# Output projection by tokens, routing by halves and 2 MB expert loads in a one-core hybrid decoder layer

## The chip, the core and the metric

The kernel runs on one core of one Trainium2 chip. It is one program that computes a whole decoder layer (token mixer, then a mixture of 32 experts) for 256 tokens of width 1024. The metric is the device time of one execution, in microseconds. Compute engines are TensorE (PE; its weight loads are shown apart as PEld), VectorE (DVE), ScalarE (ACT) and GpSimd (POOL); SyncE (SP) issues nearly all the loads from HBM, in one fixed order.

## The reference, cut to what matters

```python
# T = 256 tokens, D_MODEL = 1024, 32 experts of width 512, all f32
merged = sigmoid(gate_a) * (o_attn @ w_branch_attn) + sigmoid(gate_r) * (o_rwkv @ w_branch_rwkv)
h = h + gt1 * (merged @ w_out)                       # the output projection, 1024 x 1024
xn2 = _rmsnorm(h, moe_norm_g) * (1.0 + sc2) + sh2
# _hier_moe(xn2):
p_group = softmax(xt @ wg_router)                    # 4 groups, the best one is taken
e_logits = xt @ we_router + e_bias                   # 32 experts, the best 2 in that group
hdn = silu(xt @ wg) * (xt @ wu)                      # per expert: gate, up ...
acc = acc + cw[:, None] * (hdn @ wd)                 # ... and down
h = h + gt2 * moe
```

The output projection's result decides the routing, and the routing decides which tokens each expert sees. The weights of the experts are 3 x 2 MB for each of 32, 192 MiB (201 MB) together.

## The kernel before

**Token mixer.** Generators for modulation, selection, RWKV, attention and gates are stepped by a string written by hand (`ORDER`); each step issues a few instructions. Products are made nearly in f32: every operand is cast to the reduced type fp32r as a high part, and what the cast left is a low part. `split` (L526 to L529) does it for a tile of weights, with a cast on ACT or POOL and a subtraction on DVE or POOL (`SPLIT` says by letters which, "AP" being cast on ACT and subtraction on POOL). `mm3` (L539 to L541) then makes three products: high by high, high by low, low by high.

**Output projection.** `w_out` comes in four loads of 1 MB, `("wo", j)`, each with two of the eight slices k of the contraction. Slices are split one ahead of the other into two pairs of tiles. For every k, `out_part(m, k, w)` makes the part of one block m of 128 outputs for all 256 tokens: the weights that TensorE holds are `w[0][:, m:1024:8]`, every eighth column of the split slice, and the 256 tokens are streamed. The result is h transposed (outputs on partitions, tokens along the row), in eight blocks of 256 columns in PSUM, which four products with zeros (`zero`) open. For the last two slices the loop over m is outside, so that blocks come ready one by one; router products (`logits`, L1479), sums of squares (`squares`, L1485) and transposes back to tokens on partitions (`turn`, L1491, into `h2`) follow. To start with, the input x had been transposed into `h` in `rwkv()` (L1072).

**Routing.** A chain of small instructions on DVE (L1562 to L1593) makes 1/rms by iteration, normalises the router's sums, takes the best group and the two best experts for all 256 tokens at once; three products (L1597, L1598) rank the tokens of each expert, `places` builds a one-hot table (L1694, L1697), and `gather` (L1624) collects by products up to 32 tokens for each of four experts. `begin` (L1714) adds h into the four PSUM banks of the final sum by four 512-column products with the identity.

**Experts.** They run in eight quads of four: gate and up by `rows_in` and `row_in` (L1639, L1645: the 32 gathered tokens are the weights, 512 columns of an expert's matrix stream), down by L1666. SP's loads go in a fixed order; `pump` issues the next as soon as the arena in SBUF has a free place of its size (keeping `RESERVE` columns free in each stage), and `done` frees a tile and calls `pump`. Expert matrices of quads 0 and 1 are loaded in halves of 1 MB; from quad 2 on in 2 MB (`WHOLE = 2`), but for `down` in the last quad. The first quad's first gate halves come by slices k (`row_in`), so that each product frees some of them. Extra room comes when the split tiles of the mixer are given up (pools `more0` and `more`).

Of the kernel before, what the change touches and what calls it, by code (L numbers as in the profile page):

```python
# [18 lines left out]
D = 1024  # L19
# [34 lines left out]
RESERVE = (29696, 17408, 24576, 4096, 0)  # L54
# [4 lines left out]
SPLIT = (('PD', 'PD', 'AP', 'AD'), ('PD', 'PD', 'AP', 'AD'), ('PP', 'PP', 'AD', 'AD'), ('AD', 'AP', 'AD', 'AD'), ('AD', 'PD', 'AP', 'PD'))  # L59
PRIO = ('mod', 'sel', 'rwkv', 'attn', 'gate')  # L60
ORDER = 'mrrrrrrrrmmrmrrmrrrrrmrrrarmmrmrrmmmmrrrmarmmrmarrramrmamrrsraarmmraarmarmmaasrmmsaaaasmmsrarssrarrsaraarrararrsaasrsasssagrarssssgsraargrsrgsrsgggsrrmgmmgsmrrrrggrgrsgrrggggrsaggrrrggaggrgrrrgagagaggagaaggggaaaggaaggggaggagaggaaaagaaggaaaaaggaaaaaaggagagggggggggg'
LORD = (0, 1, 2, 3, 4, 5, 6, 7, 8, 9, 10, 13, 15, 11, 12, 14, 17, 16, 18, 23, 19, 20, 21, 22, 24, 28, 25, 27, 29, 26, 30, 31, 32, 33, 34, 35, 36, 37, 38, 44, 39, 40, 41, 51, 45, 49, 42, 48, 43, 47, 52, 46, 50)
INFO = []
QUADS = NE // 4
WHOLE = 2
# [91 lines left out]
def layer_kernel(tc, I, out, dbg=None):  # L157
# [21 lines left out]
    B = Arena(fr.__enter__().tile([128, nB], F32R, name="split"), nB)  # L179
# [83 lines left out]
    def whole(n, q):  # L263

        return q >= WHOLE and not (n == "ed" and q == QUADS - 1)

# [70 lines left out]
    nc.sync.dma_start(out=wrt[:, :, 0:4], in_=I["router_group_w"][0].rearrange("(p k) n -> p k n", p=128))  # L337
    nc.sync.dma_start(out=wrt[:, :, 4:36], in_=I["router_expert_w"][0].rearrange("(p k) n -> p k n", p=128))
# [100 lines left out]
    xhi = B.get(8, T)  # L439
    xlo = B.get(8, T)  # L440

    def mod_half(hf):
# [32 lines left out]
        def rest(kk, eng):  # L475
            k = 4 * hf + kk
            eng.tensor_sub(xlo[:, k, :], xn[:, kk, :], xhi[:, k, :].bitcast(F32))


        for kk in range(2):  # L480
            nc.scalar.activation(xhi[:, 4 * hf + 2 + kk, :], src(2 + kk), AF.Identity, scale=mo[:, 1, 2 + kk:3 + kk],
                                 bias=mo[:, 0, 2 + kk:3 + kk])
            normed(kk)
            nc.scalar.copy(xhi[:, 4 * hf + kk, :], xn[:, kk, :])  # L484
# [58 lines left out]
    def proj_cols(key, c0, ps, last=False):  # L543

        for k2 in range(2):
# [3 lines left out]
            for kk in range(4):  # L549
                k = 4 * k2 + kk  # L550
                mm3(ps, (h[:, kk, :], l[:, kk, :]), (xhi[:, k, :], xlo[:, k, :]), k == 0, k == 7)
# [12 lines left out]
    def rows_part(key, hf, mp, n, fin, i0=0):  # L564

        ps = PS(WIDE)
        for m in range(n):
# [3 lines left out]
            for i, (a, b) in enumerate(((h, xhi), (l, xhi), (h, xlo))):  # L571
                for kk in KORD:
                    nc.tensor.matmul(p, a[:, kk, :], b[:, 4 * hf + kk, :], start=(i == 0 and kk == KORD[0]),  # L573
                                     stop=(i == 2 and kk == KORD[-1]))
# [63 lines left out]
    h = io = io1 = zero = trib = selb = trib_ = selb_ = mg = m8 = rs2 = sel = comb = rk = rt = hsq = hx = None  # L638

    def rwkv():  # L640
# [396 lines left out]
        nonlocal h, io, io1, zero, trib, selb, trib_, selb_, mg, m8, rs2, sel, comb, rk, rt, hsq, hx  # L1037
        h = M(8, T)
        hx = M(1024)
        hsq = hx[:, 0:768].rearrange("p (k t) -> p k t", k=3)  # L1040
        rt = hx[:, 768:1024]
        xt = M(2, D)
        nc.sync.dma_start(out=xt, in_=I["x"][0].rearrange("(a p) d -> p a d", p=128))
# [4 lines left out]
        zero = M(64)  # L1048
        nc.gpsimd.memset(zero, 0.0)
# [17 lines left out]

        for q in range(4):
            ps = PS()
            for kk in range(2):  # L1070
                for a in range(2):
                    nc.tensor.transpose(ps[:, kk * 256 + a * 128:kk * 256 + a * 128 + 128],  # L1072
                                        xt[:, a, 2 * q + kk:D:8], ident)
            nc.scalar.copy(h[:, 2 * q:2 * q + 2, :], ps.rearrange(v2, a=2))
            yield 0.5
        A.free(xt)
# [884 lines left out]
```

## Time and the profile before

| what | before |
|---|---|
| median of 3 runs | 801.64 us (800.87 to 804.71) |
| the profiled execution | 800.6 us, its span 798.8 us |
| mean granted TensorE clock | 0.921 of 2.4 GHz |
| busy: PE, PEld, DVE, ACT, POOL | 83%, 47%, 35%, 21%, 17% of the span |
| moved by DMA | 261.36 MB, mean 327 GB/s |

The span is the time between the first and the last instruction that the profiler saw. PE's busy share is an upper figure, since a pipelined product's end is modelled; how far apart products start says more. All times below are microseconds from the start of the span.

### The profile page before, as it was taken

To read this page: it belongs to the slowest core of one execution; us is meant where nothing else is said; L and a number is where in the kernel's file an instruction comes from. 1 tells how busy PE (TensorE), PEld (TensorE's weight loads), DVE (VectorE), ACT (ScalarE), POOL (GpSimd) and SP (SyncE) were. 2 spreads that over 40 slices of the span, in tenths; PEclk is the share of its full clock that TensorE was granted. 3 is DMA by queue.
4 is the path that set the end of the run, shared out by engine and by line. 5 is a ranking of instruction groups with operands and counts; after the bars stand their busy time and mean duration, and the time that the engine had idled before them with its cause. 6 is when DMAs were issued, how large, how long until landed. Compare 5 with 4: busy or idle time off the path is not lost.

```text
span 798.8 us, 11321 instructions
## 1 busy us (share of the span) xinstructions
PE 660.6 (83%) x4657; PEld 379.2 (47%) x4657; DVE 277.0 (35%) x665; ACT 164.9 (21%) x350; POOL 132.9 (17%) x171
## 2 busy tenths in 40 slices
PE   5898988899999999989998586777676777778567
PEld 2785657568889889974442131131131132222112
DVE  2577799887255645141211061011010010010001
ACT  2445412343176631031110010010010010000000
POOL 1456643322235133220000000000000000000000
PEclk9899999999999999989999698889889899889879
DMA  9997476552758368249999999999999999999995
GB/s 334 392 309 245 143 261 241 175 192 81 244 191 284 106 235 344 66 162 377 422 420 428 427 425 431 425 427 432 425 428 429 427 427 428 427 428 427 427 394 201
DMA packets 53796, 261.36 MB, mean 327 GB/s; under 512 B 6864, under 2 KB 18128, under 8 KB 37360
## 3 DMA queue, kind: packets, MB, share of 16 engines
q1 hardware_dynamic: 53456, 260.11, 82.4%
q8 instruction: 37, 0.61, 0.3%
q10 hardware_dynamic: 288, 0.52, 0.2%
q14 instruction: 15, 0.12, 0.0%
HBM read 259.57 MB, written 1.05 MB: 326 GB/s over the span
## 4 chain that ended last, share of the span: by engine, by line
DMA 33%; PE 27%; DVE 1%; SPq 1%; POOL 1%; ACT 0%; issue 0%; ACTq 0%; POOLq 0%
DMA more<-in_expert_w_up_dram 12%; DMA more<-in_expert_w_down_dram 11%; DMA more<-in_expert_w_gate_dram 10%; PE ps_e L1639 10%; PE ps_e L1666 4%; PE ps_e L1624 2%; PE ps_a L541 1%; PE ps_a L539 1%; PE ps_a L540 1%; PE acc L1721 1%; PE ps_e L1673 1%; PE acc L1714 1%; SPq L296 1%; PE ps_r L539 0%; PE ps_r L540 0%; PE ps_r L541 0%
## 5 line engine op out<-in xcount | busy, mean ns | idle before, releaser
L1639 PE MATMUL ps_e<-arena,more 128*32 128x512 f32 x456 | 83.9, 693 | 24.2 <-DMA arena<-in_expert_w_gate_dram 18.3
L1639 PE MATMUL ps_e<-arena 128*32 128x512 f32 x424 | 81.9, 709 | 22.4 <-DMA arena<-in_expert_w_up_dram 12.4
L1666 PE MATMUL ps_e<-arena 128*32 128x512 f32 x360 | 73.5, 659 | 17.6 <-DMA arena<-in_expert_w_down_dram 12.9
L529 DVE TENSOR_TENSOR split<-arena,split 128x512 fp32r<-128x512 f32 x77 | 61.3, 805 | 57.7 <-POOL split L526 29.1
L528 ACT CAST split<-arena 128x512 fp32r<-128x512 f32 x71 | 43.3, 618 | 74.6 <-PE ps_g L540 29.3
L573 PE MATMUL ps_a<-split 128*128 128x256 f32 x360 | 52.1, 303 | 3.3 <-ACT split L484 1.9
L1650 ACT ACTIVATE arena<-ps_e 128x512 f32<-128x512 f32 x8 | 4.8, 597 | 239.2 <-PE ps_e L1639 239.2
L1651 DVE SCALAR_TENSOR_TENSOR arena<-arena,ps_e 128x512 f32<-128x512 f32 x8 | 5.5, 688 | 140.0 <-ACT arena L1650 140.0
L573 PEld LDWEIGHTS ps_a<-split 128*128 128x128 f32 x360 | 47.8, 204 | 12.6 <-issue 6.8
L529 POOL TENSOR_TENSOR split<-arena,split 128x512 fp32r<-128x512 f32 x33 | 45.3, 1372 | 48.6 <-ACT split L528 25.5
L1704 POOL TENSOR_TENSOR arena<-arena 128x256 f32<-128x256 f32 x8 | 4.9, 616 | 283.4 <-PE ps_e L1707 281.8
L1683 DVE TENSOR_TENSOR arena<-ps_e,more 128x512 f32<-128x512 f32 (+1 forms) x17 | 11.8, 692 | 112.9 <-PE ps_e L1666 103.7
L1639 PEld LDWEIGHTS ps_e<-arena,more 128*32 128x32 f32 x456 | 18.6, 126 | 60.8 <-issue 27.7
L1639 PEld LDWEIGHTS ps_e<-arena 128*32 128x32 f32 x424 | 18.2, 128 | 56.4 <-issue 26.1
L1666 PE MATMUL ps_e<-more,arena 128*32 128x512 f32 x88 | 34.9, 632 | 8.4 <-DMA more<-in_expert_w_down_dram 7.7
L526 POOL TENSOR_SCALAR split<-arena 128x512 fp32r<-128x512 f32 x39 | 26.8, 688 | 82.9 <-PE ps_r L540 23.8
L1639 PE MATMUL ps_e<-more,arena 128*32 128x512 f32 x56 | 31.3, 722 | 10.7 <-DMA more<-in_expert_w_gate_dram 10.7
L1666 PEld LDWEIGHTS ps_e<-arena 128*32 128x32 f32 x360 | 16.5, 117 | 49.0 <-issue 22.5
L1639 PE MATMUL ps_e<-more,more 128*32 128x512 f32 x56 | 30.3, 702 | 10.6 <-DMA more<-in_expert_w_up_dram 10.6
L1652 DVE SCALAR_TENSOR_TENSOR arena<-arena,ps_e 128x512 f32<-128x512 f32 x8 | 8.2, 1029 | 87.3 <-PE ps_e L1639 87.3
L539 PE MATMUL ps_g<-split 128*128 128x256 f32 x128 | 38.3, 299 | 0.0
L1624 PEld LDWEIGHTS ps_e<-arena,more 128*128 128x128 f32 x256 | 30.9, 196 | 12.9 <-issue 8.2
(379 smaller groups left out, 1263.0 us busy)
## 6 DMA issues: line engine op xcount, KB each, us to landing
arena<-in_expert_w_gate_dram SPq DMA_DIRECT2D x21, 2048.0 KB, 22.3
arena<-in_expert_w_up_dram SPq DMA_DIRECT2D x21, 2048.0 KB, 23.6
arena<-in_expert_w_down_dram SPq DMA_DIRECT2D x17, 2048.0 KB, 21.1
arena<-in_w_in_dram SPq DMA_DIRECT2D x18, 1024.0 KB, 8.1
arena<-in_expert_w_down_dram SPq DMA_DIRECT2D x18, 1024.0 KB, 17.9
arena<-in_ada_w_dram SPq DMA_DIRECT2D x16, 1024.0 KB, 6.8
arena<-in_expert_w_up_dram SPq DMA_DIRECT2D x14, 1024.0 KB, 9.8
arena<-in_expert_w_gate_dram SPq DMA_DIRECT2D x12, 1024.0 KB, 8.3
```

Source lines behind the costliest of these rows:

```text
L296: nc.sync.dma_start(out=dst, in_=src)
L526: nc.gpsimd.tensor_scalar(h, w, 1.0, 0.0, op0=OP.mult, op1=OP.add)
L528: nc.scalar.copy(h, w)
L529: (nc.gpsimd if p[1] == "P" else nc.vector).tensor_sub(l, w, h.bitcast(F32))
L539: nc.tensor.matmul(ps, l[0], r[0], start=start, stop=False)
L540: nc.tensor.matmul(ps, l[0], r[1], start=False, stop=False)
L573: nc.tensor.matmul(p, a[:, kk, :], b[:, 4 * hf + kk, :], start=(i == 0 and kk == KORD[0]), stop=(i == 2 and kk == KORD[-1]))
L1624: nc.tensor.matmul(ps[:, n * kk:n * kk + n], h2[:, a, 2 * k2 + kk, :], oh(a), start=(a == 0), stop=(a == 1))
L1639: nc.tensor.matmul(ps[32 * g:32 * g + 32, :], xg[:, k, 32 * g:32 * g + 32], w[:, k - 4 * i, :], start=(k == 0), stop=(k == 7))
L1652: nc.vector.scalar_tensor_tensor(hidb[0:r].rearrange("p (j q) -> p q j", j=4), thb[0:r].rearrange("p (q j) -> p q j", j=4), 0.5, psu[0:r, ...
L1666: nc.tensor.matmul(pss[c][32 * g:32 * g + 32, :], hTb[:, j, 32 * g:32 * g + 32], w[:, j - 2 * i, 512 * c:512 * c + 512], start=(j == 0), s ...
L1683: nc.vector.tensor_mul(Yb[0:r, c:c + 512], ps[0:r], gt2[0][0:r, g:g + 512])
```

## The change

It has four parts. **By tokens:** in the output projection the merged input (`xhi`, `xlo`, 128 tokens of it) is now what TensorE holds, and 512 columns of `w_out` stream; the result has tokens on partitions, the same way round as x, which is loaded straight into `h2`. The transposes of x, the products with zeros and the transposes back fall away; gt1 is now spread over the partitions as a row (two f32 products of 512 columns and two ACT copies more, `mod_bcast`). **By halves:** `LAST` is an order written by hand for the end of the projection: O for the products of one 128-token half and one 512-column half, T for four transposes, L for router products, N (`root`) for 1/rms and R (`route`) for the choice of one half of the tokens. W is an extra bf16 product of 512 columns that nobody reads. `CHAIN` places the four products of `begin` in the routing; `weights` (the softmax of the chosen) goes behind the first expert products and `prepare` for quad 1 behind quad 0's `down`. **Loads:** 2 MB from expert 4, counted from 0, on (`WHOLE = 1`), and in the last quad `up` in halves as well. **Memory and tables:** the split pool is cut so that 4096 columns come free after `("wo", 1)` and 6144 at the end, where before it was 2048 ahead of the projection and the rest at the end; `ORDER`, `LORD` (the order of the mixer's loads), `SPLIT` and `RESERVE` have new numbers.

```diff
-RESERVE = (29696, 17408, 24576, 4096, 0)
+RESERVE = (25600, 17408, 20480, 4096, 0)
-WHOLE = 2
+WHOLE = 1
+CHAIN = ('01', '2', '', '3', '', '')
+LAST = 'O00 O01 O10 O11 O20 O21 T00 O30 T01 L00 O31 L01 N0 R0 T10 W2 T11 N1 W1 L10 L11'
...
-        return q >= WHOLE and not (n == "ed" and q == QUADS - 1)
+        return q >= WHOLE and not (n != "eg" and q == QUADS - 1)
...
-    def out_part(m, k, w):
-        mm3(block(m), (w[0][:, m:1024:8], w[1][:, m:1024:8]), (mh[:, k, :], ml[:, k, :]), k == 0 and m > 5,
-            k == 7 and m not in (0, 2, 4))
+    def leave_room(name, cols, *before, **k):
+        for p in before:
+            p.__exit__(None, None, None)
+        state["more"].append(Arena(pool(name=name, bufs=1, **k).tile([128, cols], F32, name="more" + name), cols))
+        pump()
+
+    def out_part(a, c, k, w):
+        s = slice(128 * a, 128 * a + 128)
+        mm3(pso[2 * a + c], (xhi(k, s), xlo(k, s)), (w[0][:, 512 * c:512 * c + 512], w[1][:, 512 * c:512 * c + 512]), k == 0,
+            k == 7)
+
+    def residual(a, c):
+
+        hv = h2[:, a, 512 * c:512 * c + 512]
+        for o in (0, 256) if a and c else (0,):
+            r = slice(o, o + 256 if a and c else 512)
+            nc.vector.tensor_mul(tb[c][:, r], pso[2 * a + c][:, r], gt1[:, 512 * c:512 * c + 512][:, r])
+            (nc.vector if a else nc.gpsimd).tensor_add(hv[:, r], hv[:, r], tb[c][:, r])
+        nc.scalar.activation(tb[c], hv, AF.Square, scale=1.0 / 32, accum_out=st[:, 2 * c + a:2 * c + a + 1])
...
+            if kk:
+                done(("wo", j))
+            for n in range(4 if j < 3 else 0):
+                out_part(n // 2, n % 2, 2 * j + kk, ws[kk])
+        if j == 1:
+            leave_room("sb1", nB2 + 2048, fr2, fr1, side="right")
...
+    def warm(ps, n):
+
+        for _ in range(n):
+            nc.tensor.matmul(ps, trib[:, 0:128], trib[:, None, 0:256].to_broadcast([128, 2, 256]), start=True, stop=True)
...
+    after_last(ranks)
+    for f in CHAIN[1]:
+        after_last(lambda: begin(int(f)) if f != "W" else warm(psw, 1))
...
-                        fetch(0, [k2])
-                        for k in () if i else (2 * k2, 2 * k2 + 1):
-                            row_in(ps, XGb[0], need(("row", k)), k)
-                            done(("row", k))
+                        after_last(lambda: fetch(0, [k2]))
+                        for f in CHAIN[2 + k2]:
+                            after_last(lambda: begin(int(f)) if f != "W" else warm(psw, 1))
+                    for k in range(0 if i else 4):
+                        after_last(lambda: row_in(ps, XGb[0], need(("row", k)), k))
+                        done(("row", k))
```

On PE, the end of the output projection before: the last two products of the projection (split weights, 256 tokens), router products with 36 columns, transposes L1491, sums of squares L1485, and the ranks L1597.

```order
L540 MATMUL ps_r<-split 128x256
L541 MATMUL ps_r<-split 128x256
L1479 MATMUL ps_r<-arena 128x36 x4
L1491 MATMUL ps_g<-arena 128x128 x4
L1479 MATMUL ps_r<-arena 128x36 x4
L1491 MATMUL ps_g<-arena 128x128 x2
L1485 MATMUL ps_r<-arena 128x1 x6
L1491 MATMUL ps_g<-arena 128x128 x10
L1597 LDWEIGHTS arena
L1597 MATMUL ps_g<-arena 128x32
```

The same place after the change: L550 to L552 are the three products of the projection, L1498 transposes, L1505 router products, L1570 the products that nobody reads.

```order
L552 MATMUL ps_r<-split 128x512
L1498 MATMUL ps_g<-arena 128x128 x4
L1505 MATMUL ps_r<-arena 128x36 x4
L550 MATMUL ps_r<-split 128x512
L551 MATMUL ps_r<-split 128x512
L552 MATMUL ps_r<-split 128x512
L1505 MATMUL ps_r<-arena 128x36 x4
L1498 MATMUL ps_g<-arena 128x128 x4
L1570 LDWEIGHTS arena
L1570 MATMUL ps_r<-arena 128x512
```

Products have twice the columns; the transposes of the first half of the tokens and half of its router products stand before the projection's last products, and products that nobody reads stand behind them. Further on, between the ranks and the first expert products on PE, before:

```order
L1714 MATMUL acc_3382<-more,arena 128x512
L1624 MATMUL ps_e<-arena,more 128x128 x4
L1714 MATMUL acc_3383<-more,arena 128x512
L1645 MATMUL ps_e<-arena 32x512 x8
L1624 MATMUL ps_e<-arena,more 128x128 x7
```

And after (L1599 is `begin`, L1653 `gather`, L1674 `row_in`):

```order
L1599 MATMUL acc_3232<-arena 128x512
L1653 MATMUL ps_e<-arena 128x128 x8
L1599 MATMUL acc_3233<-arena 128x512
L1674 MATMUL ps_e<-arena 32x512 x16
L1653 MATMUL ps_e<-arena 128x128 x8
```

Eight gathering products, not four, now stand ahead of the first expert product, and all sixteen products by slices follow in one piece. On SP, the loads around this place after the change (`moresb_3057` and `moresb_3219` are the two rooms that come free):

```order
L300 DMA moresb_3057<-in_expert_w_down_dram 128x2048
L300 DMA arena<-in_expert_w_down_dram 128x2048 x2
L300 DMA moresb_3219<-in_expert_w_down_dram 128x2048 x3
L300 DMA arena<-in_expert_w_down_dram 128x2048 x2
L300 DMA arena<-in_expert_w_gate_dram 128x4096 x4
```

Before, the last of these rows stood as eight loads of 128x2048; the number of 1 MB pieces ahead of it is the same, 24, of which 22 don't wait for an expert product, in both kernels.

## Rows read from the trace of the kernel before

**Rows 1.** Page: GB/s in 40 slices of the span; the chain that ended last.

```profile
GB/s 334 392 309 245 143 261 241 175 192 81 244 191 284 106 235 344 66 162 377 422 420 428 427 425 431 425 427 432 425 428 429 427 427 428 427 428 427 427 394 201
DMA 33%; PE 27%; DVE 1%; SPq 1%; POOL 1%; ACT 0%; issue 0%; ACTq 0%; POOLq 0%
```

**Rows 2.** SP's DMA issues in order of time: start, us, queue, line, tile.

```profile
363.94 1.27 SPq L296 DMA_DIRECT2D arena<-in_expert_w_down_dram  x2
367.64 9.85 SPq L296 DMA_DIRECT2D arena<-in_expert_w_gate_dram  x8
```

**Rows 3.** Windows: busy PE, PEld, DVE, ACT, POOL (times), PEclk, DMA share, GB/s.

```profile
310.00:320.00 10.00, 10.00 (x43) 10.00 (x43) 1.99 (x3) 1.25 (x2) 2.55 (x3) 1.00 0.90 362
...
342.00:348.00 6.00, 6.00 (x35) 6.00 (x35) 2.23 (x5) 2.43 (x6) 3.64 (x5) 1.00 0.00 0
...
356.00:358.00 2.00, 0.83 (x4) 0.66 (x5) 1.63 (x14) 0.57 (x4) 0.24 (x1) 0.50 0.84 315
```

**Rows 4.** Timeline of PE: start, us, line, of the output projection's products.

```profile
300.30 0.51 PE L539 MATMUL ps_a<-split 128*128 128x256 f32 x1
...
316.06 0.41 PE L540 MATMUL ps_a<-split 128*128 128x256 f32 x1
316.30 0.40 PE L541 MATMUL ps_a<-split 128*128 128x256 f32 x1
...
348.42 0.40 PE L541 MATMUL ps_r<-split 128*128 128x256 f32 x1
```

**Rows 5.** Weight loads from 240 to 350 us by form: times, busy us, mean ns.

```profile
L539 PEld LDWEIGHTS ps_a<-split 128*128 128x128 f32 x48 | 16.2, 338 | 0.3 <-POOL split L526 0.3
...
L539 PEld LDWEIGHTS ps_g<-split 128*128 128x128 f32 x48 | 9.2, 191 | 0.3 <-issue 0.2
```

**Rows 6.** Timeline of PE: 512-column products of the same three lines, mixer.

```profile
154.34 0.39 PE L541 MATMUL ps_a<-split 128*128 128x512 f32 x1
154.57 0.40 PE L539 MATMUL ps_a<-split 128*128 128x512 f32 x1
```

**Rows 7.** Splits from 296 to 345 us, by line and form, three engines.

```profile
L529 POOL TENSOR_TENSOR split<-arena,split 128x512 fp32r<-128x512 f32 x5 | 7.4, 1489 | 1.5 <-ACT split L528 1.3
L526 POOL TENSOR_SCALAR split<-arena 128x512 fp32r<-128x512 f32 x8 | 6.1, 766 | 23.8 <-PE ps_r L540 23.8
...
L529 DVE TENSOR_TENSOR split<-arena,split 128x512 fp32r<-128x512 f32 x12 | 10.1, 867 | 23.4 <-POOL split L526 23.4
...
L528 ACT CAST split<-arena 128x512 fp32r<-128x512 f32 x8 | 5.0, 623 | 26.5 <-PE ps_r L540 26.0 <-PE ps_g L540 0.5
```

**Rows 8.** Timeline of PE in the routing, up to the first expert products.

```profile
348.66 0.98 PE L1479 MATMUL ps_r<-arena 128*128 128x36 f32 x8
349.47 0.64 PE L1491 MATMUL ps_g<-arena 128*128 128x128 f32 x4
...
357.43 2.05 PE L1714 MATMUL acc<-more,arena 128*128 128x512 f32 x2 [0.50 <-DVE arena L1608]
359.30 1.89 PE L1624 MATMUL ps_e<-arena,more 128*128 128x128 f32 x8
...
362.82 1.93 PE L1645 MATMUL ps_e<-arena 128*32 128x512 f32 x16
364.68 1.83 PE L1624 MATMUL ps_e<-arena,more 128*128 128x128 f32 x14
```

**Rows 9.** Timeline of DVE in the routing.

```profile
348.86 0.48 DVE L1519 SCALAR_TENSOR_TENSOR arena<-ps_r,arena 128x256 f32<-128x256 f32 x1 [1.41 <-PE ps_r L541]
...
352.44 0.16 DVE L1562 TENSOR_SCALAR arena<-ps_r 128x2 f32<-128x2 f32 x1 [2.56 <-PE ps_r L1485]
...
356.41 0.20 DVE L1593 TENSOR_SCALAR arena<-arena 128x64 bf16<-128x64 f32 x1
```

**Rows 10.** Windows with 1 MB loads (first row), and with 2 MB loads.

```profile
390.00:430.00 40.00, 37.25 (x279) 14.07 (x280) 5.86 (x12) 3.91 (x10) 0.79 (x2) 1.00 1.01 421
430.00:590.00 160.00, 113.56 (x618) 36.90 (x615) 27.55 (x58) 8.58 (x20) 1.85 (x3) 0.85 1.01 428
```

More of the change, by code (lines that the diff above doesn't have):

```diff
@@ L1332, in fin_a @@
         (nc.vector if s.start > 4 else nc.gpsimd).tensor_add(mgd[:, s, :], mgd[:, s, :], t)
[L1333 to L1336 removed]
+        mh, ml = (xhl[s.start // 4][:, s.start % 4:s.start % 4 + 2, i] for i in range(2))
+        nc.scalar.copy(mh, mgd[:, s, :])
+        nc.vector.tensor_sub(ml, mgd[:, s, :], mh.bitcast(F32))
     mgd = M(8, T)
@@ L1482, in squares @@
-    def squares():
-        for a in range(2):
-            for j in range(3):
-                nc.tensor.matmul(psl[:, 128 + a:129 + a], hsq[:, j, 128 * a:128 * a + 128], ones[:, 0:1], start=False, stop=(a == 1 and j == 2))
-    def turn(m):
-        pst = PS("g")
-        for a in range(2):
-            nc.tensor.transpose(pst[:, 128 * a:128 * a + 128], h[:, m, 128 * a:128 * a + 128], ident)
-        nc.scalar.copy(h2[:, :, m, :], pst[:, 0:256].rearrange("p (a c) -> p a c", a=2))
-    def block(m):
-        return pso[m // 2][:, 256 * (m % 2):256 * (m % 2) + 256] if m < 6 else pso[m - 3][:, 0:256]
@@ L1501, in layer_kernel, with turn, logits @@
+    def turn(a, c):
+        ps = PS("g")
+        for kk in range(4):
+            nc.tensor.transpose(ps[:, 128 * kk:128 * kk + 128], h2[:, a, 512 * c + 128 * kk:512 * c + 128 * kk + 128], ident)
+        nc.scalar.copy(hts[c], ps.rearrange("p (k t) -> p k t", k=4))
+    def logits(a, c):
+        for kk in range(4):
+            k = 4 * c + kk
+            nc.tensor.matmul(psl[a][:, 0:36], hts[c][:, kk, :], wrt[:, k, :], start=(k == 0), stop=(k == 7))
     cnt_split[0] += cnt_split[0] % 2
@@ L1527, in layer_kernel @@
-        done(("wo", j))
-    fr.__exit__(None, None, None)
-    state["more"].append(Arena(pool(name="sb2", bufs=1).tile([128, nB], F32, name="more"), nB))
-    h2 = state["more"][-1].get(2048, from_top=False).rearrange("p (a k c) -> p a k c", a=2, k=8)
-    turn(0)
-    turn(1)
-    logits(6)
-    turn(2)
-    logits(7)
-    squares()
-    for m in range(3, 8):
-        turn(m)
-    A.free(h)
-    A.free(gt1)
+            if kk:
+                done(("wo", j))
+            for n in range(4 if j < 3 else 0):
+                out_part(n // 2, n % 2, 2 * j + kk, ws[kk])
@@ new lines, in warm @@
+    def warm(ps, n):
+        for _ in range(n):
+            nc.tensor.matmul(ps, trib[:, 0:128], trib[:, None, 0:256].to_broadcast([128, 2, 256]), start=True, stop=True)
+    for what in LAST.split():
+        f, i = what[0], [int(c) for c in what[1:]]
+        if f == "O":
+            out_last(*i)
+        elif f in "TL":
+            after_last(lambda: (turn if f == "T" else logits)(*i))
+            if f == "L" and i[1]:
+                nc.scalar.copy(lg[:, i[0]], psl[i[0]][:, 0:36])
+        elif f == "N":
+            root(*i)
+        elif f == "W":
+            after_last(lambda: warm(psl[1], i[0]))
+        else:
+            route(*i)
@@ new lines, in layer_kernel, with begin @@
+    leave_room("sb2", nB - 2048, fr)
+    A.free(gt1, *tb)
+    pump()
+    pctx.__exit__(None, None, None)
+    state["tag"] = "e"
+    psp = pool(name="psp2", bufs=1, space=PSUM)
+    acp = pool(name="acp", bufs=1, space=PSUM)
+    acc = [acp.tile([128, 512], F32, name=f"acc{i}") for i in range(4)]
+    def begin(n):
+        nc.tensor.matmul(acc[n], ident, h2[:, n // 2, 512 * (n % 2):512 * (n % 2) + 512], start=True, stop=False)
+    psw = PS()
+    for f in CHAIN[0]:
+        after_last(lambda: begin(int(f)) if f != "W" else warm(psw, 1))
```

252 lines of the change are left out of this document (108 added, 144 removed).

## The prediction

> **What bounds the kernel now.** I read the page first. In the second half of the span DMA runs at 420 to 432 GB/s slice after slice, while the slices ahead of it move anything from 66 to 392 GB/s, and the chain that ended last is DMA for a third of the span and PE for a quarter [rows 1]. So the kernel has two halves: a first one of products and small operations, in which loads wait for room, and a stream of expert weights that saturates DMA to the end. Such a stream ends at a fixed distance from its start: what matters is when it starts. SP's issues show that [rows 2]: the loads at 363.94 wait for the first expert products (by the program each needs the place that a `row_in` tile frees), and from there on issue follows issue. The windows ahead of that show DMA doing nothing at all in 342 to 348 and PE fully busy from 310 on [rows 3]. So the stretch from the first product of the output projection, 300.30 [rows 4], to the first expert product, 362.82 [rows 8], is on the path, us for us: it is PE's for 48.4 us (300.30 to 348.66, where the last router products begin), and a chain of DVE and PE for 14.2 us.
>
> **The projection.** Inside it PE starts a product every 0.24 us [rows 4], 43 in 10 us [rows 3]. A product has 256 columns; what is slow is the weight load beside it: 338 ns with every eighth column, 191 ns for the same line and the same 128x128 from packed columns [rows 5]. 192 products at 0.24 make 46.1 us of the 48.4. After the change each product streams 512 columns, and the nearest rows are products of the same three lines with 512 columns and packed weights, one every 0.23 us [rows 6]. There are 96: 22.1 us.
>
> A rule speaks against this gain. The Trainium skill, "TensorE: Matmul & The Clock Gate", section "LDWEIGHTS (loading the stationary operand)", counts a weight load by its columns alone, and the section on weight-path modes lists weights "packed or strided" alike. By that reading stride would cost nothing, 192 products of half the columns would be as long as 96, and this term would be nothing. The rows differ by 1.8 times at one line, so I follow the rows.
>
> PE may now wait for the splits, since it is through a slice in 12 x 0.23 = 2.8 us, which was 5.8. A slice's split tiles come free when PE is through with the slice two before. One slice of two is split "AP" then "PD": ACT 0.62, POOL's subtraction 1.49, POOL's cast 0.77, DVE 0.87 [rows 7], together 3.75 us, the first 512 columns after 2.1. The second 512 columns are wanted 2.8 + 0.7 = 3.5 us after the start: a wait of 0.25, three times. The other kind ("AD", "PD") is through in about 2.4. The last two slices are taken in turns, so slice 7's first half (ACT 0.62 + DVE 0.87 = 1.5) is wanted after three products, 0.7: a wait of 0.8. I put 1.6 for these waits and 0.3 for the start. Ahead of the last product there now stand also eight transposes (four are 0.64 with the last one's end, so some 0.5 each time) and four router products, eight instructions in the trace, 0.8 (348.66 to 349.47) [rows 8]. Sum: 22.1 + 1.6 + 0.3 + 1.0 + 0.8 = 25.8 us instead of 48.4, **-22.6**. Bounds: 24 with no waits; 30 if each slice took POOL's 3.75 us.
>
> **Routing.** Before, in pieces: 3.8 us from 348.66 to DVE's first instruction at 352.44, which waited for the sums of squares; 4.2 of DVE to 356.61; 6.2 from there to the first expert product [rows 8, 9]. After: the last quarter of the result needs two multiplications and two additions of 256 columns on DVE, 4 x 0.45 by the 0.48 of such a row [rows 9], 1.8. Transposes, copy and router products of the second half (0.6 + 0.6 + 1.6) run on PE and ACT while DVE does the first half's root and choice, so DVE's chain still counts 4.2 in all, now with a wait of some 0.3 for the second half's sums. Of the 6.2, two stretches are `begin` products at half clock, ahead of the gathering (357.43 to 359.30) and behind it (361.2 to 362.82), 3.5 us [rows 8]; the granted clock was already 0.50, the lower level of 1.2 GHz, in the window of 356 to 358, in which PE was busy for 0.83 of 2 us [rows 3]. After the change one such product stands behind the gathering, 1.0 at full clock (half of the 2.05), and of the tables that the other had covered I count 0.8. The gathering is twice as many instructions: 16 at 0.13 are 2.1 (14 took 1.83), against 1.89 for 8 at half clock. So 6.2 - 3.5 + 1.0 + 0.8 + 0.2 = 4.7. Together 1.8 + 4.2 + 0.3 + 4.7 = 11.0 instead of 14.2, **-3.2**. The three products that nobody reads and three `begin` products lie in DVE's time: they cost 0.2 to 0.9 us each only if PE, not DVE, is last. Bounds: 9 if the second half's chain is hidden better, 14.5 if the clock falls all the same.
>
> **Ahead of the projection.** PE loses 16 transposes (0.12 each, 1.9) and four products with zeros (four at 0.23, 0.9), and gains two f32 products of 512 columns, about 1.0 each. That is -0.8 on an engine that was busy nearly all the time; four ACT copies go too, two ACT copies and seven POOL subtractions more than before come in. I take **-1.0**. The new `ORDER`, `LORD` and `SPLIT` tables move hundreds of instructions and the trace can't price that: I allow 4 us either way, twice what POOL's subtractions would cost if three of them (1.49 each) came to lie on the path.
>
> **Loads.** Quad 1 with 2 MB pieces: 25.2 MB at 428 instead of 421 GB/s [rows 10], 58.8 instead of 59.8 us, -1.0; the last `up` in halves, 8.4 MB, gives 0.3 back: **-0.7**. By the Trainium skill, "DMA: Bandwidth & Descriptors", section "Measured (HBM→SBUF, 128 partitions, SWDGE, issued from GpSimd)", 1 MB transfers come to 341 and 16 MB to 425 GB/s; that would make this several times larger. With many loads under way this trace shows 421 against 428, so I leave it at 0.7.
>
> Is DMA ready for an earlier start? Both kernels can issue 22 loads of 1 MB before an expert product has freed anything. The last three of them now wait for the projection's last product, near 299.3 + 25.8 = 325.1. At 428 GB/s a load is 2.45 us, so they are in by 332.5 and the earlier ones before them, while the first expert product would come at 325.1 + 11.0 = 336.1 (before 362.82). So DMA idles some 4 us; it would become the bound only if the chain gained that much more. The memory parts of the change cost nothing here, since that idle time covers them; without it each load that comes late costs its 2.45.
>
> **Sum.** The stream starts 22.6 + 3.2 + 1.0 = 26.8 us earlier, and is 0.7 shorter: -27.5. The profiled execution took 800.6, 1.0 under the median: 773.1 for such an execution, **774** for the median.
>
> **The rivals.**
> *The splits or the mixer give some back.* POOL makes 3.75 us of work out of each second slice where PE wants one every 2.8; if POOL is late from the mixer's end (it is in the waits just ahead of 300), each slice is late by one more, and the projection takes 30: 778. With the mixer 4 us later, 782. For it: POOL's 1.49 us rows. Against: the first half-slices are ready earlier than they are wanted.
> *The routing is not shorter.* If PE's chain of the second half (transposes, copy, router products, then choice) ends last, or the clock falls to 1.2 GHz as it did, 3 to 4 us go: 777. For it: two chains in a row on DVE. Against: PE has work in the gaps.
> *The stride is not what made the loads slow.* Then 96 products take what 192 took, and only routing and loads are left: 800.6 - 4.9, or 796 to 797 for the median. Against: 0.23 for 512 columns in the same kernel.
> *Slower: the stream starves on 2 MB pieces.* A 2 MB load needs two neighbouring free places, and SP's queue is in order, so one that waits holds all behind it. Each 2 MB of missing cover costs up to 4.9 us. With the first tiles of quad 0 freed singly, quad 1 could wait for pairs; it decides from six such holes on (27.5 / 4.9), and gives some 808 with seven. Against: quads 2 to 7 stream 2 MB pieces at a share of 1.01 without a hole [rows 10].
>
> **How the numbers follow.** The likeliest, 0.66: the sum as it stands, 768 to 780 by the bounds of its terms (projection 24 to 30, routing 9 to 14.5, mixer 4 either way, not all on one side). Splits or mixer giving back more, or the routing, 0.22 together: 776 to 787. Stride not the cause, 0.03. Slower by starving, or by a mixer that slips by more than the gain, 0.05. What is left, 0.04, is smaller gains near no change. The range of 765 to 786 leaves out the last three cases and little of the second. A measurement of this kernel tells about 0.5% from no change: faster by more than that 0.92, within it 0.03, slower 0.05.
>
> **What would show it.** In the changed profile: weight loads in the projection near 190 ns and products every 0.23 us; waits of PE for DVE or POOL splits under 3 us in all; the last product of the projection at 325 and the first expert product at 336, three us either way; the granted clock 1.00 between them; DMA idle for some us just before, then 420 to 430 GB/s without a hole to the end, in quad 1 too. Wrong it would be if products stood at 0.3 us or more, if the projection started later than 304, or if a slice of the stream fell under 410 GB/s between 340 and 750.

## The result

The changed kernel takes 777.1 us (median of 4, 776.0 to 778.3) against 802.2 us (median of 4): 0.968 of the time, 95% interval 0.965 to 0.971, or 25 us less. Forecast were 774 us, in a range of 765 to 786.

The page of the profile after: its span, and GB/s in 40 slices, to hold against [rows 1].

```profile
span 774.6 us, 11047 instructions
...
GB/s 332 387 311 236 167 282 239 212 170 89 258 260 192 110 218 250 416 299 409 382 425 426 430 427 428 427 427 429 426 429 427 427 428 425 429 431 423 423 393 199
```

The shape is the same: an uneven first part, then a stream at 423 to 431 GB/s up to its last two slices. Its beginning moved up by more than a slice; the slice of 349 to 368 us moves 409 GB/s and that of 368 to 387 us only 382. The timeline of PE after (start, us, line): first and last product of the projection, gathering (L1653), first expert products (L1674).

```profile
295.89 0.39 PE L550 MATMUL ps_a<-split,split 128*128 128x512 f32 x1
...
300.00 0.40 PE L550 MATMUL ps_a<-split,split 128*128 128x512 f32 x1
301.71 0.50 PE L551 MATMUL ps_a<-split,split 128*128 128x512 f32 x1 [1.32 <-DVE split L540]
...
323.43 0.40 PE L552 MATMUL ps_r<-split 128*128 128x512 f32 x1
...
331.67 4.07 PE L1653 MATMUL ps_e<-arena 128*128 128x128 f32 x16 [0.24 <-DVE arena L1721]
335.58 1.02 PE L1599 MATMUL acc<-arena 128*128 128x512 f32 x2
336.53 3.64 PE L1674 MATMUL ps_e<-arena 128*32 128x512 f32 x32
```

The projection starts 4.4 us earlier than in [rows 4] and lasts 27.8 us (295.89 to 323.67, with 0.24 for the last product), where it was 48.4. From there to the first expert product it is 12.9 us, where it was 14.2 [rows 8]. SP's issues after, against [rows 2]:

```profile
337.74 1.19 SPq L300 DMA_DIRECT2D arena<-in_expert_w_down_dram  x2
340.31 11.69 SPq L300 DMA_DIRECT2D arena<-in_expert_w_gate_dram  x4
...
384.96 2.00 SPq L300 DMA_DIRECT2D arena<-in_expert_w_down_dram  x4
```

The first loads that expert products release come at 337.74 and not 363.94: 26.2 us earlier. The span is only 24.2 shorter. So the stream itself, from there to the end, takes 436.9 where it took 434.9. Windows after (busy PE, PEld, DVE, ACT, POOL, then PEclk, DMA share, GB/s), with the hole that SP's issue at 384.96 ends:

```profile
332.00:336.00 4.00, 4.00 (x17) 3.77 (x17) 1.29 (x4) 0.16 (x1) 0.62 (x1) 1.00 0.41 166
384.00:388.00 4.00, 4.00 (x26) 2.55 (x14) 0.80 (x2) 0.60 (x1) 0.00 (x0) 1.00 0.70 205
```

In the first window DMA runs dry while PE gathers, in the second PE is busy all the time and DMA is not. And the lines by which to see why PE is late: the gathering's weight loads in the changed kernel, first, and in the kernel before (L1624); then those of the projection in the changed kernel (least, median and most ns).

```profile
L1653 PEld LDWEIGHTS ps_e<-arena 128*128 128x128 f32 x256 | 62.1, 334 | 12.8 <-issue 6.7
```

```profile
L1624 PEld LDWEIGHTS ps_e<-arena,more 128*128 128x128 f32 x256 | 30.9, 196 | 12.9 <-issue 8.2
```

```profile
L550 PEld LDWEIGHTS ps_r<-split,split x4: 187/188/188, 298.4 to 309.0; 128*128 128x128 f32 x4
L550 PEld LDWEIGHTS ps_r<-split x4: 187/189/192, 311.8 to 322.9; 128*128 128x128 f32 x4
```

With the result kept with tokens on partitions in natural order, the gathering now takes every eighth column (`h2[:, a, 2 * k2 + kk:D:8]`) as weights. The load that had been 338 ns in the projection [rows 5] is gone there, and has come in here.

### The profile page after: what moved, and what is told of

Same layout as the page of the kernel before. It is cut to its first block, busy times and chain, and to the rows that moved or that the text cites. A ratio compares the mean times of both kernels' runs of the same rounds, so it can differ in the third digit from the quotient of the medians.

```text
span 774.6 us, 11047 instructions
## 1 busy us (share of the span) xinstructions
PE 659.0 (85%) x4534; PEld 378.8 (49%) x4534; DVE 272.7 (35%) x662; ACT 166.6 (22%) x351; POOL 137.0 (18%) x169
## 4 chain that ended last, share of the span: by engine, by line
PE 45%; DMA 34%; DVE 8%; POOL 5%; issue 3%; SPq 3%; ACT 2%; POOLq 0%; DVEq 0%; ACTq 0%
PE ps_e L1668 11%; DMA arena<-in_expert_w_down_dram 9%; DMA arena<-in_expert_w_gate_dram 8%; DMA moresb<-in_expert_w_gate_dram 7%; PE ps_e L1653 5%; DMA arena<-in_expert_w_up_dram 4%; DMA moresb<-in_expert_w_up_dram 4%; PE ps_a L584 3%; PE ps_g L550 3%; PE ps_g L551 3%; PE ps_g L552 3%; SPq L300 2%; PE ps_e L1695 2%; PE ps_g L461 2%; POOL arena L595 1%
## 5 line engine op out<-in xcount | busy, mean ns | idle before, releaser
L1668 PE MATMUL ps_e<-arena 128*32 128x512 f32 x752 | 149.7, 656 | 30.9 <-DMA arena<-in_expert_w_gate_dram 27.9
L1695 PE MATMUL ps_e<-arena 128*32 128x512 f32 x352 | 78.9, 671 | 22.4 <-DMA arena<-in_expert_w_down_dram 18.0
L1668 PE MATMUL ps_e<-moresb,arena 128*32 128x512 f32 x240 | 86.4, 683 | 10.7 <-DMA moresb<-in_expert_w_gate_dram 6.4
L1668 PEld LDWEIGHTS ps_e<-arena 128*32 128x32 f32 x752 | 35.7, 119 | 99.1 <-issue 54.6
L1653 PEld LDWEIGHTS ps_e<-arena 128*128 128x128 f32 x256 | 62.1, 334 | 12.8 <-issue 6.7
L1653 PE MATMUL ps_e<-arena 128*128 128x128 f32 x256 | 64.9, 408 | 0.2 <-DVE arena L1721 0.2
L540 POOL TENSOR_TENSOR split<-arena,split 128x512 fp32r<-128x512 f32 x39 | 51.6, 1325 | 59.1 <-ACT split L539 48.1
L1712 DVE TENSOR_TENSOR arena<-ps_e,arena 128x512 f32<-128x512 f32 (+1 forms) x17 | 11.8, 691 | 121.7 <-PE ps_e L1695 108.8
L1695 PEld LDWEIGHTS ps_e<-arena 128*32 128x32 f32 x352 | 18.6, 118 | 71.9 <-issue 35.3
L1695 PE MATMUL ps_e<-moresb,arena 128*32 128x512 f32 x96 | 42.9, 674 | 3.4 <-DMA moresb<-in_expert_w_down_dram 2.6
L1668 PEld LDWEIGHTS ps_e<-moresb,arena 128*32 128x32 f32 x240 | 19.4, 123 | 47.3 <-issue 28.0
L550 PE MATMUL ps_g<-split,split 128*128 128x256 f32 x128 | 37.5, 293 | 0.0
L551 PE MATMUL ps_g<-split,split 128*128 128x256 f32 x128 | 36.2, 283 | 0.0
L552 PE MATMUL ps_g<-split,split 128*128 128x256 f32 x128 | 36.1, 282 | 0.0
L1738 PE MATMUL acc<-arena 128*128 128x512 f32 (+1 forms) x68 | 31.9, 608 | 0.8 <-DVE arena L1712 0.8
```

The lines of the kernel that those rows point to most:

```text
L540: (nc.gpsimd if p[1] == "P" else nc.vector).tensor_sub(l, w, h.bitcast(F32))
L550: nc.tensor.matmul(ps, l[0], r[0], start=start, stop=False)
L551: nc.tensor.matmul(ps, l[0], r[1], start=False, stop=False)
L552: nc.tensor.matmul(ps, l[1], r[0], start=False, stop=stop)
L1653: nc.tensor.matmul(ps[:, n * kk:n * kk + n], h2[:, a, 2 * k2 + kk:D:8], oh(a), start=(a == 0), stop=(a == 1))
L1668: nc.tensor.matmul(ps[32 * g:32 * g + 32, :], xg[:, k, 32 * g:32 * g + 32], w[:, k - 4 * i, :], start=(k == 0), stop=(k == 7))
```

## The experiments

Theory 1: a weight load with a stride of eight costs 335 ns instead of 190 wherever it stands; the projection was slow by it and the gathering now is. Rivals: the projection gained because it has half as many products; the hole comes from the 2 MB pieces. In the table, all from the traces: start of the projection's first product, from the start of its last product to the first expert product, SP's first issue behind an expert product, and from there to the end of the span. A median is to be held against the changed kernel of its group; the last row against the kernel before, which took 802.8 us beside it.

| run | median us | projection starts | last product to experts | first released load | stream |
|---|---|---|---|---|---|
| before | 802.2 | 300.30 | 14.4 | 363.94 | 434.9 |
| changed | 777.1 | 295.89 | 13.1 | 337.74 | 436.9 |
| changed, group 1 | 777.9 | 298.92 | 13.1 | 340.72 | 436.4 |
| gathering packed | 771.8 | 297.41 | 11.1 | 337.23 | 433.4 |
| no extra products | 778.4 | 297.82 | 13.1 | 339.68 | 436.8 |
| `begin` late | 778.7 | 296.10 | 12.4 | 338.10 | 439.1 |
| changed, group 2 | 777.3 | 297.29 | 13.1 | 339.13 | 436.4 |
| quad 1 in 1 MB | 776.1 | 297.38 | 13.1 | 339.24 | 435.4 |
| before, weights packed | 779.2 | 300.06 | 14.1 | 341.30 | 434.9 |

**The changed kernel again**, twice, as yardstick. 

> The changed kernel once more, unchanged, as the yardstick for the three others of this group, since they differ from it by a few us at most. Both theories: 0.968 of the kernel before, 776 to 778 us.

 

> The changed kernel once more, unchanged, as the yardstick for the others of this group. Both theories: 0.968 of the kernel before, 776 to 778 us.

 They came out at 0.970 and 0.969 (intervals 0.967 to 0.972 and 0.967 to 0.971). The projection's start differs by 3 us between profiles of one and the same kernel; the first released load moves with it, and the other two columns repeat within 0.5.

**The kernel before with packed weights.**

```diff
-        mm3(block(m), (w[0][:, m:1024:8], w[1][:, m:1024:8]), (mh[:, k, :], ml[:, k, :]), k == 0 and m > 5,
+        mm3(block(m), (w[0][:, 128 * m:128 * m + 128], w[1][:, 128 * m:128 * m + 128]), (mh[:, k, :], ml[:, k, :]), k == 0 and m > 5,
```

> The kernel before, but out_part takes 128 neighbouring columns of the split weights for block m and not every eighth one (so the outputs come in another order); still 192 products of 256 columns. Theory 1 (the stride of the weights cost the projection its time): weight loads near 191 ns, a product every 0.12 us where the splits are ready, so 23 us of products; the splits (up to 3.75 us a slice against 2.9 of products) then add 2 to 5: the projection falls from 48.4 to 26 to 30 us, and the time by 18 to 22 us, 780 to 784. Rival (the number of products and weight loads cost it, and 512 columns brought the gain): weight loads near 191 ns or not, a product still every 0.2 us or more, and the time above 790 us.

 The kernel leaves out putting the outputs back in order, so it prices the stride and can't replace the change. Measured: 779.2 us, 0.970 (0.966 to 0.974). The timeline of PE, and weight loads by form from 295 to 350 us:

```profile
300.06 0.28 PE L539 MATMUL ps_a<-split 128*128 128x256 f32 x1
300.17 0.28 PE L540 MATMUL ps_a<-split 128*128 128x256 f32 x1
...
326.07 0.28 PE L541 MATMUL ps_r<-split 128*128 128x256 f32 x1
```

```profile
L539 PEld LDWEIGHTS ps_a<-split 128*128 128x128 f32 x48 | 9.2, 192 | 0.0
```

Still 192 products, one every 0.12 us, and 26.1 us for the projection (300.06 to 326.19). One slice of an index makes the projection 22 us shorter and the median 23.6, slightly more than theory 1 expected; the rival is out. The rewrite by tokens needs 27.8 us for the same place, 2.5 of it for transposes and router products that stood behind it before: fewer and longer products gained next to nothing over packed weights.

**The gathering packed, in the changed kernel.**

```diff
-                    nc.tensor.matmul(ps[:, n * kk:n * kk + n], h2[:, a, 2 * k2 + kk:D:8], oh(a), start=(a == 0),
+                    nc.tensor.matmul(ps[:, n * kk:n * kk + n], h2[:, a, 128 * (2 * k2 + kk):128 * (2 * k2 + kk) + 128], oh(a), start=(a == 0),
```

> The gathering's weights are read as 128 neighbouring columns of h2 and not as every eighth column, so the experts get tokens with their columns in another order; all else is the same. Theory 1 (the stride was only moved: it left the projection and came into the gathering, whose weight loads are now 335 ns where they were 192, and this is on the path): weight loads near 190 ns, 16 gathering instructions in about 2.1 us instead of 3.9, the first expert product 1.5 to 2 us earlier, and the hole in the stream of loads near 385 us smaller or gone; 773 to 775.5 us. Rival (the gathering is hidden, and the hole comes from the 2 MB pieces of the second quad): no more than 0.5 us faster, the hole stays.

 The kernel leaves out the right order of the columns, which the experts' matrices need. Measured: 771.8 us, 0.963 (0.960 to 0.965) against 0.970 (0.967 to 0.972) for the changed kernel beside it. Timeline of PE, SP's issue that ended the hole, and the window of the hole:

```profile
333.18 2.05 PE L1653 MATMUL ps_e<-arena 128*128 128x128 f32 x16 [0.24 <-DVE arena L1721]
335.07 1.02 PE L1599 MATMUL acc<-arena 128*128 128x512 f32 x2
336.02 3.64 PE L1674 MATMUL ps_e<-arena 128*32 128x512 f32 x32
```

```profile
378.38 1.75 SPq L300 DMA_DIRECT2D arena<-in_expert_w_down_dram  x4
```

```profile
384.00:388.00 4.00, 3.88 (x29) 1.04 (x31) 0.86 (x3) 1.07 (x3) 0.62 (x1) 1.00 1.02 434
```

16 instructions take 1.9 us and not 3.9, the first expert product comes 2.0 earlier, and the hole is gone: the stream is 3.0 to 3.5 us shorter. The load that ends the hole goes 42.4 us behind the first expert product (378.38 less 336.02), where it went 48.4 behind it (384.96 less 336.53): the gatherings of quads 0 and 1 had made PE 6 us late. A smaller dip goes too: 12 to 16 us behind the first expert product DMA moves 426 GB/s here and 332 in the changed kernel, worth some 0.9 us. Theory 1 had undersized it: 6.1 us by the medians where 2 to 4.5 were expected; the trace accounts for 5.0 to 5.5 of them.

**Quad 1 in pieces of 1 MB** (`WHOLE = 2`). 

> Quad 1 is loaded in pieces of 1 MB again (2 MB from the ninth expert on, as before the change); all else as in the changed kernel. Theory 1 (2 MB pieces give 428 instead of 421 GB/s over one quad, and the hole near 385 us comes from the gathering, not from the size): 0.5 to 1 us slower. Rival (the 2 MB pieces make the hole of about 2 us near 385 us, since each waits for two neighbouring places): the hole is gone, and it is 1 to 2 us faster.

 Measured: 776.1 us, 0.967 (0.966 to 0.969) against 0.969 (0.967 to 0.971) beside it. The window of the hole:

```profile
384.00:388.00 4.00, 4.00 (x31) 1.57 (x24) 0.08 (x1) 0.60 (x1) 0.00 (x0) 1.00 1.01 422
```

The hole is gone too, but the smaller dip stays (334 GB/s), and 1 MB pieces move 421 GB/s where 2 MB pieces move 428 [rows 10], which costs some 1.0 us for the quad; so the stream is 1.0 shorter and not 2. The medians differ by 1.2 with intervals that overlap, so the trace says more here than the time. The hole needs both: PE late by the gathering, and pieces so large that the next load waits for a late product. Either alone doesn't make it.

**No extra products** (`W2` and `W1` out of `LAST`). 

> The three bf16 products that nobody reads are left out. Theory 1 (they only fill time in which PE waits for VectorE and ScalarE): nothing, within 0.5 us, and the granted clock stays at 1.00 in the routing because router products, transposes and the products that begin the sum still stand there. Rival (they keep the clock up): the granted clock falls to 0.50 somewhere between 325 and 345 us, the gathering and the first expert products take up to twice as long, 1.5 to 4 us slower. A third: they delay the last router products by up to 0.6 us, and it gets that much faster.

 Measured: 778.4 us, 0.972 (0.969 to 0.975) against 0.970 (0.967 to 0.972). Windows of the routing:

```profile
324.00:328.00 4.00, 3.94 (x29) 3.25 (x30) 3.52 (x20) 2.24 (x6) 0.00 (x0) 1.00 1.01 412
328.00:332.00 4.00, 3.71 (x20) 2.49 (x20) 3.44 (x29) 1.90 (x9) 0.00 (x0) 1.00 0.99 397
332.00:336.00 4.00, 3.75 (x16) 2.81 (x15) 2.37 (x14) 0.40 (x2) 0.85 (x2) 1.00 0.86 360
```

The granted clock stays at 1.00 (2.4 GHz), and the way to the experts is 13.1 us with or without them. They do nothing that can be measured.

**The products of `begin` all late** (`CHAIN = ('', '', '', '', '', '0123')`). 

> The four products that begin the sum all stand behind the gathering and the first expert products, so that none lies in the routing. Theory 1 (one of the four, between gathering and expert products, is on the path for 1.0 us, the others fill idle time; the clock stays): first expert product 1.0 us earlier, 0.5 to 1 us faster or the same. Rival (they are what keeps the clock up between 326 and 332 us): granted clock 0.50 in the gathering, whose 16 instructions then take up to 5 us or more, and 1 to 4 us slower.

 Measured: 778.7 us, 0.971 (0.969 to 0.974). Windows, the gathering on PE, and, last, the third window in the changed kernel:

```profile
328.00:332.00 4.00, 0.72 (x7) 0.44 (x6) 3.43 (x26) 1.48 (x7) 0.24 (x1) 0.93 1.00 420
332.00:336.00 4.00, 4.00 (x16) 3.81 (x16) 1.48 (x6) 0.00 (x0) 0.61 (x1) 0.50 0.45 186
...
350.00:360.00 10.00, 10.00 (x89) 3.19 (x78) 1.97 (x3) 1.08 (x3) 0.62 (x1) 1.00 0.74 280
```

```profile
331.89 4.21 PE L1653 MATMUL ps_e<-arena 128*128 128x128 f32 x16 [1.20 <-DVE arena L1721]
```

```profile
350.00:360.00 10.00, 9.27 (x74) 3.20 (x70) 1.43 (x2) 2.04 (x4) 0.61 (x1) 1.00 0.98 403
```

Here PE is busy for 0.72 of 4 us, the granted clock falls to 0.50 (1.2 GHz), as in the kernel before [rows 3], and the gathering runs at it. It takes 4.1 us (331.89 to 336.03), hardly more than the 3.9 at 1.00: with strided columns the lower clock costs it little. The first expert product comes 0.7 earlier all the same, but the four products then stand in the expert work and DMA is idle for a quarter of 350 to 360. Both theories had a part. From the last product to the end of the span this profile is 2.4 to 2.9 us longer (553.6 against 551.2 and 550.7); the medians differ by 0.8, with intervals that overlap. In these two runs it is the `begin` products, not the unread ones, that hold the clock.

**The tables of the kernel before** (ORDER, LORD, SPLIT, RESERVE), with 2 MB and with 1 MB pieces in quad 1. 

> ORDER, LORD, SPLIT and RESERVE as in the kernel before; projection, routing and loads as in the changed one. Theory 1 (the mixer is 4.4 us shorter by the new tables mostly, only 1 us of it by the transposes that are gone): the projection starts 2.5 to 4 us later, at 298.5 to 300, and the time is 779 to 781 us. Rival (the tables do nothing, the removed transposes and copies gave it all): the projection starts within 1 us of 295.9, and the time is within 1 us.

 

> The tables ORDER, LORD, SPLIT and RESERVE of the kernel before, as in the run that was 6 us slower, and quad 1 in pieces of 1 MB. Theory 1 (with the old tables the tiles lie so that the first 2 MB piece waits for two neighbours, and that made the 6 us): 776.5 to 779 us. Rival (the 6 us come from one load less ahead of the first expert products, or from the mixer): 781 us or more.

 Measured: 783.3 us, 0.977 (0.974 to 0.979), and 781.0 us, 0.972 (0.969 to 0.975). The projection starts at 297.96 in the first profile and at 301.21 in the second; in the ten profiles with the new tables it starts between 295.89 and 298.92. Two executions don't settle whether the tables shorten the mixer, and the second speaks for it. SP's issues in the first; then PE's first product and a window in the second:

```profile
327.31 14.54 SPq L300 DMA_DIRECT2D arena<-in_expert_w_down_dram  x4
349.84 0.81 SPq L300 DMA_DIRECT2D arena<-in_expert_w_gate_dram  x2
```

```profile
301.21 0.39 PE L550 MATMUL ps_a<-split,split 128*128 128x512 f32 x1
```

```profile
330.00:332.00 2.00, 2.00 (x9) 1.45 (x8) 1.44 (x8) 1.37 (x4) 0.00 (x0) 0.51 0.85 221
```

The first 2 MB piece goes at 349.84, 11.2 us behind the first expert product, where it went 3.8 behind it (340.31) after the change, and one load less stands ahead of the expert products. From the first expert product to the end it takes 439.9 and 439.1 us, where the new tables take 437.6 with 2 MB and 436.6 with 1 MB pieces: 2.3 and 2.5 more, about one load (2.45 in the prediction). The 1 MB pieces give back 0.8 there, so theory 1, that the pieces made the 6 us, is out. The rest of the 6 us lies ahead of that or in executions that were not profiled (those profiled took 780.3 and 784.2), and no run here decides it. In the second profile the granted clock also fell to 0.51 in 330 to 332, with the unread products in place, after PE had been busy for 1.43 of 2 us in 326 to 328 and for all of 328 to 330; the way to the experts is 14.6 us there and not 13.1. Why it fell is not shown.

**Outputs permuted in the split.** The split reads w_out in the order of the gathering, so that its weights are packed. The line of the split is shown; the residual, `begin`, the gathering and the router's tables change with it.

```diff
-                split(w[:, kk:kk + 1, 512 * hh:512 * hh + 512])
+                split(w[:, kk, :].rearrange("p (c k) -> p k c", k=8)[:, 4 * hh:4 * hh + 4, :])
```

> The outputs of the projection are put in the order k by c when the weights are split (the casts and subtractions read w_out at a stride of 8 and write packed), and the result stays in that order: the weights of the projection and of the gathering are both packed, and the products that begin the sum stream with a stride. Everything is computed. Theory 1 (stride costs on the side of the weights alone): weight loads near 190 ns in both, the first expert product 1.5 to 2 us earlier than in the changed kernel, 773 to 775.5 us. Rival (a stride costs wherever it stands: the splits, additions and streamed products get slower by as much): casts and subtractions of the split take clearly over 0.62 and 0.87 us, PE waits for them, and the time is 777 us or more.

 Measured: 790.0 us, 0.984 (0.982 to 0.986). Splits from 295 to 352 us, by form, against [rows 7]:

```profile
L540 DVE TENSOR_TENSOR split<-arena,split 128x512 fp32r<-128x512 f32 x12 | 17.0, 1458 | 8.6 <-POOL split L537 8.6
L537 POOL TENSOR_SCALAR split<-arena 128x512 fp32r<-128x512 f32 x8 | 11.3, 1427 | 0.0
L539 ACT CAST split<-arena 128x512 fp32r<-128x512 f32 x7 | 8.3, 1184 | 13.9 <-PE ps_a L552 10.8 <-DMA arena<-in_expert_w_up_dram 3.1
```

The rival holds: a stride of eight f32 makes the cast 1184 instead of 623 ns on ACT, 1427 instead of 766 on POOL, and the subtraction 1458 instead of 867 on DVE. The projection takes 40 us (297.05 to 337.05). The way from its last product to the experts grows to 18.4 us, where it was 13.1, with a granted clock of 0.50 in 340 to 350; what of that is the stride in the additions, and what the clock, is not separated.

**The result copied into order by GpSimd**, in four copies while it has nothing else to do; the gathering reads neighbouring columns of the copies. Once with 2 MB and once with 1 MB pieces in quad 1.

```diff
+    hp = [[gt1[:, 0:512], tb[0]], [gt1[:, 512:1024], tb[1]]]
...
+        if c:
+            for i in range(2):
+                nc.gpsimd.tensor_copy(hp[a][i].rearrange("p (k c) -> p k c", k=4),
+                                      h2[:, a, :].rearrange("p (c k) -> p k c", k=8)[:, 4 * i:4 * i + 4, :])
```

> The changed kernel, with four copies more on GpSimd, which has nothing to do between 321 and 330 us: they put the result into the order k by c (into the places of gt1 and of a temporary), and the gathering reads 128 neighbouring columns of that. h2 is freed when the sum has begun; one load of 1 MB less can be issued ahead of it. Everything is computed. Theory 1 (the gathering's stride costs about 6 us by the run with packed columns, 2 ahead of the first expert product and the rest in the second quad's hole): copies of about 1.4 us each that end by 331 us, weight loads near 190 ns, 772 to 774.5 us. Rival (the copies are late or slow VectorE down, and the missing load makes DMA wait): first expert product no earlier, 776 us or more.

 

> As the run with the four copies, and quad 1 in pieces of 1 MB again. Theory 1 (2 MB pieces were bad only because PE was late; with PE on time they are as good): within 1 us of the run with the four copies. Rival (1 MB pieces start the stream of the second quad sooner in any case): 1 to 2 us faster than it.

 One thing in the two expectations does not hold: the first tokens' copies go into places that the second half's residual still uses, so values are lost, and that residual has to wait for them; instructions, loads and sizes are those meant. Measured: 776.6 us, 0.967 (0.964 to 0.970), and 777.2 us, 0.968 (0.965 to 0.971). Timelines of POOL and of DVE, and a window:

```profile
320.81 2.17 POOL L1499 COPY arena<-arena 128x512 f32<-128x512 f32 x2
326.21 2.17 POOL L1499 COPY arena<-arena 128x512 f32<-128x512 f32 x2 [3.24 <-DVE arena L1558]
```

```profile
321.98 0.15 DVE L1553 TENSOR_SCALAR arena<-arena 128x1 int32<-128x1 int32 x1
322.05 0.14 DVE L1555 TENSOR_SCALAR arena<-arena 128x1 f32<-128x1 f32 x1
323.01 0.69 DVE L1494 TENSOR_TENSOR arena<-ps_a,arena 128x512 f32<-128x512 f32 x1 [0.82 <-POOL arena L1499]
...
326.07 0.15 DVE L1558 SCALAR_TENSOR_TENSOR arena<-arena 128x1 f32<-128x1 f32 x1
326.26 1.09 DVE L1557 SCALAR_TENSOR_TENSOR arena<-arena 128x1 f32<-128x1 f32 x1
327.38 1.02 DVE L1558 SCALAR_TENSOR_TENSOR arena<-arena 128x1 f32<-128x1 f32 x1
328.43 0.15 DVE L1559 TENSOR_SCALAR arena<-arena 128x1 f32<-128x1 f32 x1
```

```profile
332.00:336.00 4.00, 3.11 (x13) 2.31 (x13) 2.50 (x17) 0.75 (x4) 0.85 (x2) 0.73 0.02 6
```

The copies are quick (1.09 us each), but during each of the last two DVE is held in one instruction of a single column for as long. The first two hold it in another way: at 323.01 it has waited 0.82 us for them, since they write what it needs next. DVE's chain is the path here. The choice of the experts ends 2.2 us later than in the changed kernel, counted from the last product; 1.7 of it stand in the two held instructions, and whether the wait adds the rest is not separated. PE has little to do meanwhile, its granted clock is 0.73 in 332 to 336, the gathering takes 3.4 us where it took 1.9 with packed columns alone, and the first expert product comes 14.9 us after the last product, not 11.1. The hole near 385 is gone, and the two cancel. The rival's "slow VectorE down" was the larger part. With 1 MB pieces it is within 1 us, as theory 1 of that run expected; by the traces 2 MB pieces make the stream 1.3 us shorter here (435.7 against 437.0).

## Why the prediction was right, point by point

**The projection, -22.6 forecast, -20.6 measured.** The mechanism was right, and the run with packed weights shows it alone. The rows, not the rule of the Trainium skill ("TensorE: Matmul & The Clock Gate", section "LDWEIGHTS (loading the stationary operand)"), held: two loads of 128 columns differ by 1.75 times. The Trainium skill, "SBUF — State Buffer", section "Door 1: The DMA port swizzle (why `[64,N]` ≈ `[32,N]`)", has a rule that fits, that reads which cross into a new 16-byte line at each element cost more, a stride of up to 4 f32 being free. The strides of eight here agree, in weight loads (192 against 335 ns) and in casts (623 against 1184); no run here has a shorter stride, so what is free is not shown. Mis-sized were the waits, 1.6 + 0.3 forecast. PE waits for splits almost only in the first 10 us, where DVE and POOL still finish the mixer: products stand 0.5, 1.5 and 0.5 us further apart there, and later ones 0.1. The profile gives the waits themselves (us, times, longest):

```profile
PE ps_a L551 <- DVE split L540: 1.9, 3, 1.3
```

Transposes and router products ahead of the last product took 2.5 and not 1.8, 0.6 of it a wait for ACT's copy.

**Routing, -3.2 forecast, -1.3 measured: the step that failed.** The prediction took "16 at 0.13 are 2.1" for the gathering from a row with packed columns, though the change makes the gathering read `h2` with a stride: 3.9 us. With that stride away the way is 11.1 us from the start of the last product, 10.9 from its end, against 11.0 forecast. Of the rest of that sum, one `begin` product on the path and the clock at 1.00 were right. Its other parts were off by up to 0.5 each and cancel by luck: there the last residual takes 1.5 us (1.8 forecast), DVE's chain with its wait 5.0 (4.5), and from there to the experts it is 4.3 (4.7).

**Ahead of the projection, -1.0 forecast:** -4.4 in the profile after, -1.4 and -3.0 in the repeats. The projection's start moves by 3 us from one execution to the next, the old tables gave 297.96 and 301.21, and no run separates tables, removed transposes and chance. The cause of this term stays open.

**Loads, -0.7 forecast, +1.5 to +2.0 measured.** "The memory parts of the change cost nothing here" looked at the start of the stream alone. All but the first half of quad 0's gathering is under the stream, and what quads 0 and 1 gather made PE late, with 2 MB pieces to wait for it. It is the "starves on 2 MB pieces" rival in small: one hole of some 2 us and a dip of 0.9. The gain from larger pieces was there, 1.3 us in the runs with copies, which have no hole. One of the signs of being wrong came with it: two slices between 340 and 750 us moved under 410 GB/s (409 and 382).

**Sum.** Projection, routing and loads fell short by 2.0, 1.9 and 2.7 us in this profile, and the mixer gave 3.4 more; that leaves the 3 us between 774 and 777. So the sum came this close partly by luck: without the 3.4 us that the mixer gave beyond its forecast, and whose cause is open, it would have missed by more than 6.

## What to carry to other kernels

When an operand changes its layout, look up every reader of it, on every engine, and price each by a row with the same stride; a cost that leaves one line can come back in another. A load that is slow for its size is worth one index before a rewrite: packed weights alone took 22 us off the projection, though they leave the outputs in another order. And an engine with nothing to do isn't free to use: two copies on GpSimd held VectorE, which was on the path, for 1.7 us.

## What the runs showed of the hardware

A stride of eight f32 costs 1.7 to 1.9 times on weight loads (335 against 192 ns), on ACT's and POOL's casts (1184 against 623, 1427 against 766) and on DVE's subtraction (1458 against 867). At such a stride the gathering's 16 instructions took 4.1 us at a granted clock of 0.50 and 3.9 at 1.00.

Under two POOL copies of 128x512, DVE instructions that take 0.15 to 0.22 us elsewhere took 1.0 to 1.1 us. By the Trainium skill, "SBUF — State Buffer", section "SBUF: two separate sides", GpSimd and an instruction of VectorE with two SBUF inputs take turns at one pair of ports, whole instructions at a time. This trace agrees: both held instructions have two such inputs, and two with one input took 0.15 and 0.14 us under such copies.

Three bf16 products that nobody reads changed neither clock nor time. With them in place, the granted clock fell to 0.50 in one profile after PE had been busy for only 0.72 of 4 us, and to 0.51 in another after 1.43 of 2 us and then 2 of 2.
